# Hard-max attention: three buffers for keys and queries, the next batches' loads and key differences moved to earlier tiles, and one more value gather ahead of the tail

## The chip, the cores and the metric

One core of one Trainium2 chip. The metric is the device time of one execution in microseconds (us), lower is better. A number such as "443.31 us" is the median of several executions on the chip; a "span" is the time from the first to the last instruction of the one execution that was profiled, and is some 2 us shorter. Runs are compared with runs of the kernel before on the same chip and in the same rounds.

## The reference

```python
def setup_inputs():
    B, Sq, Sk, D = 4, 4096, 4096, 128
    # q, k, v: standard normal, float32

def reference(q, k, v):
    logits = np.matmul(q, k.transpose(0, 2, 1))
    best = np.argmax(logits, axis=-1)
    b_idx = np.arange(q.shape[0])[:, None]
    return v[b_idx, best, :].astype(np.float32)
```

For each query: find the key with the largest dot product and copy out that key's value row.

## The kernel before

The queries are worked off in 128 tiles of 128 queries, 32 tiles to a batch. For one tile, PE multiplies queries with sums and differences of keys in groups of four, ACT and DVE fold the results (`W`), and DVE's MAX8 picks the best group (`TOP`). A group holds four keys, so POOL gathers the three *differences* of the group's keys (`kg`, from `k16` in HBM), DVE multiplies them with the query (`prod`) and finds the best of the four. POOL then gathers the value row (`vr`), which SP stores. At the end, queries that were too close to call are worked out again exactly (`FK`, `FQ`, `FV`), and one last scatter writes their rows. All instructions stand in a fixed order for each engine.

Three helpers matter here. They all issue their transfers from POOL, or feed one that does:

```python
natk = [bp.tile([P, 2, 16, P], FP16, ...) for i in range(2)]     # keys of a batch, natural layout
natq = [bp.tile([P, NQT, P], FP16, ...) for i in range(2)]       # queries of a batch

def load_k(b, h, x, y):                                          # float32 in HBM to fp16 in SBUF
    kb = k[b].rearrange("(h p n) d -> p h n d", p=P, n=16)
    nc.gpsimd.dma_start(out=natk[b % 2][:, h, x:y], in_=kb[:, h, x:y])

def put_first(b, h):                       # DVE negates the group's first key; SP writes it three times
    ...
    nc.vector.tensor_scalar(out=kd[:, h, :, 0, :], in0=src[:, :, 0, :], scalar1=-1.0, ...)
    for f in range(3):
        nc.sync.dma_start(out=kb16[:, h, :, f, :], in_=kd[:, h, :, 0, :])

def add_rest(b, h):                        # POOL adds the other three keys to it, in HBM
    ...
    nc.gpsimd.dma_start(out=kb16[...], in_=src[:, :, 1:4, :]..., accum_op=OP.add)
```

and the place of each in the loop over the tiles:

```python
for it in range(T):                        # T = 128
    b, qt = it // NQT, it % NQT            # NQT = 32
    if it < 8:
        load_part(1, it, 4)                # batch 1: keys in 8 pieces of 128 KB
    elif 10 <= qt < 18 and qt % 2 == 0:
        load_part(b + 1, qt - 2)       # next batch: queries in 4 pieces of 256 KB
    elif 18 <= qt < 26 and qt % 2 == 0:
        load_part(b + 2, qt - 18)      # the one after: keys in 4 pieces of 256 KB
    ...
    if it % NQT in (9, 13):
        put_first(it // NQT + 1, it % NQT // 13)
    if it % NQT in (13, 17):
        add_rest(it // NQT + 1, it % NQT // 17)
    ...
    issue(it)                              # how many value gathers POOL issues in this tile
```

`LATE = 4` is the number of value gathers that are issued ahead of the first `FK` of the tail; the rest follow it. Sizes of loads here and below are those of what they write, in fp16.

Of the kernel before, what the change touches and what calls it, by code (L numbers as in the profile page):

```python
# [8 lines left out]
FP16 = mybir.dt.float16  # L9
# [12 lines left out]
TAU = 8.0  # L22
NEAR = 0.5
SLOTS = 6
LATE = 4
NKG = 6


# [1 line left out]
def kernel(ctx, tc, q, k, v, out):  # L30
    nc = tc.nc
    B, Sq, D = q.shape
    Sk = k.shape[1]
    P = 128
    NQT = Sq // P
# [10 lines left out]
    bp = ctx.enter_context(tc.tile_pool(name="kq", bufs=1))  # L46
# [10 lines left out]
    k16 = [dr.tile([Sk, 96], FP16, name=f"k16_{b}") for b in range(B)]  # L57
    kT = [bp.tile([P, Sk], FP16, name=f"kT{i}", tag=f"kT{i}") for i in range(2)]
    qT = [bp.tile([P, Sq], FP16, name=f"qT{i}", tag=f"qT{i}") for i in range(2)]
    natk = [bp.tile([P, 2, 16, P], FP16, name=f"natk{i}", tag=f"natk{i}") for i in range(2)]  # L60
    kd = bp.tile([P, 2, 4, 3, P], FP16, name="kd", tag="kd")
    natq = [bp.tile([P, NQT, P], FP16, name=f"natq{i}", tag=f"natq{i}") for i in range(2)]

    def load_k(b, h, x, y):
        kb = k[b].rearrange("(h p n) d -> p h n d", p=P, n=16)
        nc.gpsimd.dma_start(out=natk[b % 2][:, h, x:y], in_=kb[:, h, x:y])  # L66

    def load_q(b, x, y):
        nc.gpsimd.dma_start(out=natq[b % 2][:, x:y], in_=q[b].rearrange("(p t) d -> p t d", p=P)[:, x:y])  # L69

    def put_k(b, h):
        if b >= B:
            return
        src = natk[b % 2][:, h].rearrange("p (g f) d -> p g f d", f=4)
        nc.vector.tensor_tensor(out=kd[:, h], in0=src[:, :, 1:4, :], in1=src[:, :, 0:1, :].to_broadcast([P, 4, 3, P]),
                                op=OP.subtract)
        kb16 = k16[b].rearrange("(h p n) d -> p h (n d)", p=P, n=16)
        nc.sync.dma_start(out=kb16[:, h], in_=kd[:, h].rearrange("p g f d -> p (g f d)"))

    def put_first(b, h):  # L80
        if b >= B:
            return
        src = natk[b % 2][:, h].rearrange("p (g f) d -> p g f d", f=4)
        nc.vector.tensor_scalar(out=kd[:, h, :, 0, :], in0=src[:, :, 0, :], scalar1=-1.0, scalar2=None, op0=OP.mult)
        kb16 = k16[b].rearrange("(r x) d -> r (x d)", x=4).rearrange("(h p g) (f d) -> p h g f d", h=2, p=P, f=3)
        for f in range(3):
            nc.sync.dma_start(out=kb16[:, h, :, f, :], in_=kd[:, h, :, 0, :])

    def add_rest(b, h):
        if b >= B:  # L90
            return
        src = natk[b % 2][:, h].rearrange("p (g f) d -> p g f d", f=4)
        kb16 = k16[b].rearrange("(r x) d -> r (x d)", x=4).rearrange("(h p g) (f d) -> p h g f d", h=2, p=P, f=3)
        nc.gpsimd.dma_start(out=kb16[:, h].rearrange("p g f d -> p g (f d)"), in_=src[:, :, 1:4, :].rearrange("p g f d -> p g (f d)"),
                            accum_op=OP.add)

    def load_part(b, i, n=8):
        if b >= B:
            return
        if i < 8:  # L100
            load_k(b, i // 4, i % 4 * 4, i % 4 * 4 + n)
        else:
            load_q(b, (i - 8) * NQT // 8, (i - 8 + n // 4) * NQT // 8)

    load_k(0, 0, 0, 16)
    load_q(0, 0, 4)

# [13 lines left out]
    identh = cp.tile([P, P], FP16, tag="identh")  # L121
# [73 lines left out]
    def unit_k(b, i):  # L195
        h, u, y = i // 8, i // 2 % 4, i % 2
        x = 2 * (u // 2)
        ps = pp.tile([P, 256], FP32, tag="u", name=f"uk_{b}_{i}")
        for m in (2 * y, 2 * y + 1):
            o = ps[:, (m - 2 * y) * P:(m - 2 * y + 1) * P]  # L200
            nc.tensor.matmul(out=o, lhsT=natk[b % 2][:, h, 4 * m + x, :], rhs=identh, start=True, stop=False)  # L201
            nc.tensor.matmul(out=o, lhsT=natk[b % 2][:, h, 4 * m + x + 1, :],  # L202
                             rhs=identn if u % 2 else identh, start=False, stop=True)
        c = u * 1024 + h * 512 + y * 256
        nc.scalar.activation(out=kT[b % 2][:, c:c + 256], in_=ps, func=AF.Copy)  # L205

    def turn_q(b, x, y):
        nc.sync.dma_start_transpose(out=qT[b % 2][:, x * P:y * P].rearrange("p (t r) -> p t r", r=P),
                                    in_=natq[b % 2][:, x:y, :].rearrange("p t d -> p (t d)"))

    def trn_q(x, y, put):
        ps = pp.tile([P, 512], FP32, tag="u", name=f"tq_{x}")
# [77 lines left out]
    def dots(c, x, m):  # L290
        c0 = chunks[c][0]
        d = D_t[c % 4]
        b = x // NQT
        gap = ("wait", 1) if m == 4 and x < 200 else ("dve",)
        yield "until", lambda: ("kg", x) in done, 2 if m < 4 and x < TAIL else 1
        kg = kg_t.pop(x)
        prod = rp.tile([P, 4, 3, P], FP16, tag="prod", name=f"prod_{x}")[:, 0:m]
        h = min(m, 2)
        for i in range(0, m, h):
            nc.vector.tensor_tensor(out=prod[:, i:i + h], in0=kg[:, i:i + h],  # L300
                                    in1=natq[b % 2][:, x + i - b * NQT:x + i + h - b * NQT, :].unsqueeze(2).to_broadcast([P, h, 3, P]),
                                    op=OP.mult)
            yield gap
        p1 = rp.tile([P, 4, 3, 64], FP16, tag="p1", name=f"p1_{x}")[:, 0:m]
        nc.vector.tensor_tensor(out=p1, in0=prod[:, :, :, 0:64], in1=prod[:, :, :, 64:128], op=OP.add)  # L305
        yield gap
        p2 = rp.tile([P, 4, 3, 32], FP16, tag="p2", name=f"p2_{x}")[:, 0:m]
        nc.vector.tensor_tensor(out=p2, in0=p1[:, :, :, 0:32], in1=p1[:, :, :, 32:64], op=OP.add)  # L308
        yield "dve",
        nc.vector.tensor_reduce(out=d[:, x - c0:x - c0 + m, 1:4], in_=p2, axis=AX_X, op=OP.add)  # L310
        done.update(("dot", i) for i in range(x, x + m))
# [154 lines left out]
    def flags_last(t0, t1, ready, fill, late):  # L466
# [47 lines left out]

        late(LATE)
        get(FK[:, 0, :], k_flat, gb[:, 0:1], B * Sk)
# [226 lines left out]
    def issue(it):  # L743
        n = 0
        clock[0] = it
        put_out(it)
        behind = len([g for g in near_q if g not in marks]) > (2 if it >= TAIL else 4)
        while near_q and (n < 1 + behind or near_q[0] in marks or it >= T - 1):
            g = near_q.pop(0)
            n += g not in marks  # L750
            g()
        if fast and it >= rest[0]:
            fast.pop(0)()
            rest[0] = it + 2
            n += 1
        if it < 16:
            take_late(2 if n == 0 and len(late_q) > 4 else 1)
            return
        b, qt = it // NQT, it % NQT
        busy = 0.7 if qt % 2 == 0 and (10 <= qt < 18 and b + 1 < B or 18 <= qt < 26 and b + 2 < B) else 0.0  # L760
        if qt in (13, 17) and b + 1 < B:
            busy += 1.0
        rate = 2.42 if it < 72 else 2.5 if it < 100 else 2.42
        room[0] = min(room[0] + rate - busy, 3.0) - n
        for i in range(2):
            if room[0] >= 1 and late_q and it < T - 1:
                take_late(1)
                room[0] -= 1
# [16 lines left out]
            start(flag_segment(0, t + 1, lambda: ("cnt", last) in done, lambda: ("out", last) in done), "flags")  # L785

    TAIL = T - 54
    units = []
    for b in range(1, B):
        x = b * NQT  # L790
        units += [(x - 1, x - NQT + (6 + 3 * i // 2 if b == 1 else 1 + 2 * i), unit_k, b, i) for i in range(16)]
    for it in range(T):
        b, qt = it // NQT, it % NQT
        if it < 8:
            load_part(1, it, 4)
        elif 10 <= qt < 18 and qt % 2 == 0:
            load_part(b + 1, qt - 2)
        elif 18 <= qt < 26 and qt % 2 == 0:
            load_part(b + 2, qt - 18)
        open_units = [u for u in units if u[1] <= it]  # L800
        if open_units:
            u = min(open_units)
            units.remove(u)
            assert it <= u[0]
            u[2](*u[3:])
        if it == 1:
            turn_q(0, 4, 8)
        if it == 40:
            nc.sync.dma_start(out=q32, in_=q[B - 1].rearrange("(p t) d -> p t d", p=P)[:, NQT - 2:NQT])
        if it in (1, 2, 3):  # L810
            turn_q(0, it * 8, it * 8 + 8)
        elif qt >= 16 and qt % 2 == 0 and b + 1 < B:
            turn_q(b + 1, (qt - 16) * 2, (qt - 14) * 2)
        if it > 0:
            screen(it)
        if it >= 1:
            fold(it - 1)
        if it == 1:
            put_k(0, 1)
        if it % NQT in (9, 13):  # L820
            put_first(it // NQT + 1, it % NQT // 13)
        if it % NQT in (13, 17):
            add_rest(it // NQT + 1, it % NQT // 17)
        step(it)
        if it >= 2:
            top(it - 2)
        step(it)
        if it >= 2:
            gathers(it - 2)
        issue(it)  # L830
# [75 lines left out]
```

## Time and profile before

| before | |
|---|---|
| median of 3 executions | 443.31 us (443.29 to 443.79) |
| span of the profiled execution | 441.9 us |
| DVE busy, 45 to 400 us | 353.68 of 355 us |
| transfers issued by POOL | 309 (252 of them gathers of `kg` and `vr`, 34 loads, 6 accumulates) |
| waits of `prod` for a gather | 1, of 0.4 us |
| last MAX8 starts | 405.51 us |
| from there to the final scatter | 32.1 us |
| from the final scatter to the end of the span | 4.2 us |

The prediction below shows the stages and waits, and timelines (start, duration, what, and in brackets idle time before it and what ended it). The groups of POOL's work: line, engine, operation, what it writes from what, count, then busy us in total and mean ns of one, then idle time ahead of it.

```profile
L282 POOL DMA_INDIRECT kg<-k,cand x126 | 126.4, 1003 | 80.0 <-DVE cand L276 48.7 <-issue 29.8 <-DMA vr<-in_v_dram,win 0.6
L342 POOL DMA_INDIRECT vr<-in_v_dram,win x126 | 125.9, 999 | 40.0 <-issue 36.1 <-DVE win L333 1.8 <-DMA vr<-in_v_dram,win 1.2
L66 POOL DMA_DIRECT2D natk<-in_k_dram x19 | 11.3, 599 | 0.8 <-POOLq L890 0.8
L94 POOL DMA_DIRECT2D k<-natk x6 | 8.1, 1352 | 0.0
```

A gather occupies POOL for 1.0 us, a load for 0.6, an accumulate (`k<-natk`) for 1.35. These are the times to *issue* a transfer; the bytes move later, on POOL's one queue (q0 of the trace, 19072 pieces). Then the timeline of POOL at a place that the change touches (start, duration, what, and in brackets idle time before it and what ended it):

```profile
84.56 0.95 POOL L282 DMA_INDIRECT kg<-k,cand  x1 [0.30 <-issue]
85.81 0.97 POOL L342 DMA_INDIRECT vr<-in_v_dram,win  x1 [0.30 <-issue]
86.79 0.60 POOL L66 DMA_DIRECT2D natk<-in_k_dram  x1
87.70 0.98 POOL L282 DMA_INDIRECT kg<-k,cand  x1 [0.30 <-issue]
```

### The profile page before, as it was taken

To read this page: it belongs to the slowest core of one execution; us is meant where nothing else is said; L and a number is where in the kernel's file an instruction comes from. 1 tells how busy PE (TensorE), PEld (TensorE's weight loads), DVE (VectorE), ACT (ScalarE), POOL (GpSimd) and SP (SyncE) were. 2 spreads that over 40 slices of the span, in tenths; PEclk is the share of its full clock that TensorE was granted. 3 is DMA by queue.
4 is the path that set the end of the run, shared out by engine and by line. 5 is a ranking of instruction groups with operands and counts; after the bars stand their busy time and mean duration, and the time that the engine had idled before them with its cause. 6 is when DMAs were issued, how large, how long until landed. Compare 5 with 4: busy or idle time off the path is not lost.

```text
span 441.9 us, 6163 instructions
## 1 busy us (share of the span) xinstructions
PE 378.9 (86%) x1830; PEld 168.0 (38%) x1830; DVE 405.9 (92%) x734; ACT 375.6 (85%) x437; POOL 306.2 (69%) x335
## 2 busy tenths in 40 slices
PE   7999999999999999999998889999889997892100
PEld 4444444444444444444443334443333333330100
DVE  2688999999999999999999999999999999999840
ACT  2899999999999999999998889999989998892000
POOL 8413456677768786777777776777777777777673
PEclk9999999999999999999999999999999999998555
DMA  7933999463326999743336993453322332323432
GB/s 123 202 101 65 157 148 139 106 130 80 108 58 134 180 163 170 147 114 91 84 94 142 173 162 100 96 132 107 85 82 84 90 89 80 88 80 102 122 113 53
DMA packets 52868, 50.54 MB, mean 114 GB/s; under 512 B 34136, under 2 KB 40890, under 8 KB 52832
## 3 DMA queue, kind: packets, MB, share of 16 engines
q0 software_dynamic: 19072, 33.87, 39.2%
q1 hardware_dynamic: 33760, 16.26, 14.5%
q8 instruction: 14, 0.23, 0.2%
q14 instruction: 22, 0.18, 0.2%
HBM read 40.05 MB, written 14.55 MB: 124 GB/s over the span
## 4 chain that ended last, share of the span: by engine, by line
ACT 37%; issue 20%; DVE 13%; PE 12%; POOL 8%; DMA 8%; POOLq 0%; ACTq 0%; DVEq 0%; SPq 0%
ACT A L234 31%; ACT E L247 6%; DVE TOP L264 4%; PE psn L225 4%; POOL vr L342 4%; PE pd L225 4%; POOL kg L282 4%; DVE W L260 4%; PE psn L244 3%; DMA vr<-in_v_dram,win 3%; DMA natk<-in_k_dram 2%; DMA out_dram<-vr 1%; DMA kg<-k,cand 1%; DVE prod L300 1%; DMA vr<-in_v_dram,win_w 1%
## 5 line engine op out<-in xcount | busy, mean ns | idle before, releaser
L234 ACT ACTIVATE A<-pd 128x1024 f16<-128x1024 f32 x256 | 260.8, 1046 | 12.5 <-PE pd L225 12.0
L282 POOL DMA_INDIRECT kg<-k,cand x126 | 126.4, 1003 | 80.0 <-DVE cand L276 48.7
L260 DVE SCALAR_TENSOR_TENSOR W<-psn,E 128x1024 int16<-128x1024 f32 x128 | 167.1, 1306 | 7.4 <-ACT E L247 5.3
L225 PE MATMUL psn<-kT,qT 128*128 128x512 f16 x512 | 151.9, 378 | 11.4 <-ACT A L234 4.0
L225 PE MATMUL pd<-kT,qT 128*128 128x512 f16 x512 | 151.9, 379 | 8.7 <-ACT A L234 8.2
L264 DVE MAX8 TOP<-W 128x8 f32<-128x1024 f32 x128 | 157.0, 1227 | 0.0
L225 PEld LDWEIGHTS <-qT 128*128 128x128 f16 x1024 | 97.9, 97 | 151.8 <-issue 62.0
L342 POOL DMA_INDIRECT vr<-in_v_dram,win x126 | 125.9, 999 | 40.0 <-issue 36.1
L244 PE MATMUL psn<-A,identh 128*128 128x512 f16 x512 | 152.1, 378 | 0.0
L247 ACT ACTIVATE E<-psn 128x1024 int16<-128x1024 f32 x128 | 132.6, 1036 | 2.3 <-PE psn L244 1.5
L244 PEld LDWEIGHTS <-identh 128*128 128x128 f16 x512 | 49.6, 97 | 60.7
L300 DVE TENSOR_TENSOR prod<-kg,natq 128x768 f16<-128x768 f16 x63 | 34.8, 554 | 0.4 <-DMA kg<-k,cand 0.4
L205 ACT ACTIVATE kT<-uk 128x256 f16<-128x256 f32 x48 | 20.6, 429 | 1.5 <-PE uk L202 1.5
L305 DVE TENSOR_TENSOR p<-prod 128x768 f16<-128x768 f16 (+1 forms) x36 | 18.1, 502 | 0.1
L310 DVE TENSOR_REDUCE D<-p 128x12 f32<-128x384 f16 (+1 forms) x36 | 17.7, 492 | 0.1
L201 PE MATMUL uk<-identh,natk 128*128 128x128 f16 x96 | 15.8, 218 | 0.0
L484 PE MATMUL fp_e<-n_e,tri 128*128 128x1 f32 x2 | 0.6, 364 | 13.5 <-DVE n_e L482 13.5
L202 PEld LDWEIGHTS <-natk 128*128 128x128 f16 x96 | 9.3, 97 | 7.2 <-issue 5.1
L308 DVE TENSOR_TENSOR p<-p 128x384 f16<-128x384 f16 (+1 forms) x36 | 11.9, 330 | 0.1
L66 POOL DMA_DIRECT2D natk<-in_k_dram x19 | 11.3, 599 | 0.8 <-POOLq L890 0.8
L201 PEld LDWEIGHTS <-natk 128*128 128x128 f16 x96 | 9.3, 98 | 5.6
L69 POOL DMA_DIRECT2D natq<-in_q_dram x15 | 9.2, 614 | 0.0
(152 smaller groups left out, 140.1 us busy)
## 6 DMA issues: line engine op xcount, KB each, us to landing
out_dram<-vr SPq DMA_DIRECT2D x31, 256.0 KB, 2.1
natq<-in_q_dram POOLq DMA_DIRECT2D x12, 256.0 KB, 5.3
natk<-in_k_dram POOLq DMA_DIRECT2D x10, 256.0 KB, 4.5
k<-kd SPq DMA_DIRECT2D x18, 128.0 KB, 3.7
k<-natk POOLq DMA_DIRECT2D x6, 384.0 KB, 6.4
kg<-k,cand POOLq DMA_INDIRECT x126, 3.0
vr<-in_v_dram,win POOLq DMA_INDIRECT x126, 2.7
natk<-in_k_dram POOLq DMA_DIRECT2D x8, 128.0 KB, 5.7
```

The lines of the kernel that those rows point to most:

```text
L201: nc.tensor.matmul(out=o, lhsT=natk[b % 2][:, h, 4 * m + x, :], rhs=identh, start=True, stop=False)
L205: nc.scalar.activation(out=kT[b % 2][:, c:c + 256], in_=ps, func=AF.Copy)
L225: nc.tensor.matmul(out=ps[:, n * 512:(n + 1) * 512], lhsT=qT[b % 2][:, qt * P:(qt + 1) * P], rhs=kT[b % 2][:, u * 1024 + n * 512:u * 1024 ...
L234: nc.scalar.activation(out=A, in_=ps, func=AF.Abs)
L244: nc.tensor.matmul(out=ps[:, n * 512:(n + 1) * 512], lhsT=identh, rhs=A[:, n * 512:(n + 1) * 512], start=False, stop=True)
L247: nc.scalar.activation(out=E, in_=ps, func=AF.Relu, scale=QSCALE)
L260: nc.vector.scalar_tensor_tensor(out=W_t[t % NW].bitcast(I16)[:, 1::2], in0=ps, scalar=QSCALE, in1=E, op0=OP.mult, op1=OP.max)
L264: nc.vector.max(out=TOP[:, t, :], in_=W_t[t % NW].bitcast(FP32))
L282: near_q.append(lambda j=j: nc.gpsimd.indirect_dma_start(out=kg[:, j].rearrange("p f d -> p (f d)"), out_offset=None, in_=k16[t0 // NQT], ...
L300: nc.vector.tensor_tensor(out=prod[:, i:i + h], in0=kg[:, i:i + h], in1=natq[b % 2][:, x + i - b * NQT:x + i + h - b * NQT, :].unsqueeze(2 ...
L305: nc.vector.tensor_tensor(out=p1, in0=prod[:, :, :, 0:64], in1=prod[:, :, :, 64:128], op=OP.add)
L342: late_q.append(lambda j=j: nc.gpsimd.indirect_dma_start(out=vr[:, j, :], out_offset=None, in_=v_flat, in_offset=IOA(ap=win[:, i + j:i + j ...
```

## The change

The intent: POOL looks loaded from 45 us on and has little to do in the first tiles, so work that can be done early is put there. A third buffer for keys and for queries lets the loads run further ahead. Batch 1 is loaded in four pieces of 512 KB (in tiles 0 to 3) instead of eight of 128 KB (keys) and four of 256 KB (queries); batch 2 is loaded from tile 6 on and batch 3 from tile 24 on, instead of 18 and 50; the negations and accumulates move to earlier tiles; and one more value gather is issued ahead of `FK`.

```diff
-LATE = 4
+LATE = 5
...
-    natk = [... for i in range(2)]
+    natk = [... for i in range(3)]
-    natq = [... for i in range(2)]
+    natq = [... for i in range(3)]
...            (every b % 2 of natk and natq becomes b % 3)
+    plan = {}
+    def load_plan(b, first, gap, n, what):
+        for i in range(32 // n):
+            x, y = i * n, i * n + n
+            plan.setdefault(first + i * gap, []).append(
+                lambda b=b, x=x, y=y: load_k(b, x // 16, x % 16, x % 16 + n) if what == "k" else load_q(b, x, y))
...            (in issue(): busy and rate follow the new places)
+    load_plan(1, 0, 1, 16, "k")
+    load_plan(1, 2, 1, 16, "q")
+    load_plan(2, 6, 2, 8, "k")
+    load_plan(2, 14, 2, 8, "q")
+    load_plan(3, 24, 3, 8, "k")
+    load_plan(3, 44, 4, 8, "q")
...
-        if it < 8:
-            load_part(1, it, 4)
-        elif 10 <= qt < 18 and qt % 2 == 0:
-            load_part(b + 1, qt - 2)
-        elif 18 <= qt < 26 and qt % 2 == 0:
-            load_part(b + 2, qt - 18)
+        for piece in plan.get(it, []):
+            piece()
...
-        if it % NQT in (9, 13):
-            put_first(it // NQT + 1, it % NQT // 13)
-        if it % NQT in (13, 17):
-            add_rest(it // NQT + 1, it % NQT // 17)
+        for b1, x, y in ((1, 5, 9), (2, 17, 21), (3, 38, 42)):
+            for h in range(2):
+                if it == x + 2 * h:
+                    put_first(b1, h)
+                if it == y + 2 * h:
+                    add_rest(b1, h)
```

More of the change, by code (lines that the diff above doesn't have):

```diff
@@ L59 @@
     qT = [bp.tile([P, Sq], FP16, name=f"qT{i}", tag=f"qT{i}") for i in range(2)]
-    natk = [bp.tile([P, 2, 16, P], FP16, name=f"natk{i}", tag=f"natk{i}") for i in range(2)]
+    natk = [bp.tile([P, 2, 16, P], FP16, name=f"natk{i}", tag=f"natk{i}") for i in range(3)]
     kd = bp.tile([P, 2, 4, 3, P], FP16, name="kd", tag="kd")
-    natq = [bp.tile([P, NQT, P], FP16, name=f"natq{i}", tag=f"natq{i}") for i in range(2)]
+    natq = [bp.tile([P, NQT, P], FP16, name=f"natq{i}", tag=f"natq{i}") for i in range(3)]
     def load_k(b, h, x, y):
         kb = k[b].rearrange("(h p n) d -> p h n d", p=P, n=16)
-        nc.gpsimd.dma_start(out=natk[b % 2][:, h, x:y], in_=kb[:, h, x:y])
+        nc.gpsimd.dma_start(out=natk[b % 3][:, h, x:y], in_=kb[:, h, x:y])
     def load_q(b, x, y):
-        nc.gpsimd.dma_start(out=natq[b % 2][:, x:y], in_=q[b].rearrange("(p t) d -> p t d", p=P)[:, x:y])
+        nc.gpsimd.dma_start(out=natq[b % 3][:, x:y], in_=q[b].rearrange("(p t) d -> p t d", p=P)[:, x:y])
     def put_k(b, h):
@@ L73, in put_k @@
             return
-        src = natk[b % 2][:, h].rearrange("p (g f) d -> p g f d", f=4)
+        src = natk[b % 3][:, h].rearrange("p (g f) d -> p g f d", f=4)
         nc.vector.tensor_tensor(out=kd[:, h], in0=src[:, :, 1:4, :], in1=src[:, :, 0:1, :].to_broadcast([P, 4, 3, P]),
@@ L82, in put_first @@
             return
-        src = natk[b % 2][:, h].rearrange("p (g f) d -> p g f d", f=4)
+        src = natk[b % 3][:, h].rearrange("p (g f) d -> p g f d", f=4)
         nc.vector.tensor_scalar(out=kd[:, h, :, 0, :], in0=src[:, :, 0, :], scalar1=-1.0, scalar2=None, op0=OP.mult)
@@ L91, in add_rest @@
             return
-        src = natk[b % 2][:, h].rearrange("p (g f) d -> p g f d", f=4)
+        src = natk[b % 3][:, h].rearrange("p (g f) d -> p g f d", f=4)
         kb16 = k16[b].rearrange("(r x) d -> r (x d)", x=4).rearrange("(h p g) (f d) -> p h g f d", h=2, p=P, f=3)
@@ L95, in add_rest @@
                             accum_op=OP.add)
-    def load_part(b, i, n=8):
-        if b >= B:
-            return
-        if i < 8:
-            load_k(b, i // 4, i % 4 * 4, i % 4 * 4 + n)
-        else:
-            load_q(b, (i - 8) * NQT // 8, (i - 8 + n // 4) * NQT // 8)
+    plan = {}
[4 more added lines that the diff above has]
+                lambda b=b, x=x, y=y: load_k(b, x // 16, x % 16, x % 16 + n) if what == "k" else load_q(b, x, y))
     load_k(0, 0, 0, 16)
@@ L200, in unit_k @@
             o = ps[:, (m - 2 * y) * P:(m - 2 * y + 1) * P]
-            nc.tensor.matmul(out=o, lhsT=natk[b % 2][:, h, 4 * m + x, :], rhs=identh, start=True, stop=False)
-            nc.tensor.matmul(out=o, lhsT=natk[b % 2][:, h, 4 * m + x + 1, :],
+            nc.tensor.matmul(out=o, lhsT=natk[b % 3][:, h, 4 * m + x, :], rhs=identh, start=True, stop=False)
+            nc.tensor.matmul(out=o, lhsT=natk[b % 3][:, h, 4 * m + x + 1, :],
                              rhs=identn if u % 2 else identh, start=False, stop=True)
@@ L208, in turn_q @@
         nc.sync.dma_start_transpose(out=qT[b % 2][:, x * P:y * P].rearrange("p (t r) -> p t r", r=P),
-                                    in_=natq[b % 2][:, x:y, :].rearrange("p t d -> p (t d)"))
+                                    in_=natq[b % 3][:, x:y, :].rearrange("p t d -> p (t d)"))
     def trn_q(x, y, put):
@@ L300, in dots @@
             nc.vector.tensor_tensor(out=prod[:, i:i + h], in0=kg[:, i:i + h],
-                                    in1=natq[b % 2][:, x + i - b * NQT:x + i + h - b * NQT, :].unsqueeze(2).to_broadcast([P, h, 3, P]),
+                                    in1=natq[b % 3][:, x + i - b * NQT:x + i + h - b * NQT, :].unsqueeze(2).to_broadcast([P, h, 3, P]),
                                     op=OP.mult)
@@ L759, in issue @@
         b, qt = it // NQT, it % NQT
-        busy = 0.7 if qt % 2 == 0 and (10 <= qt < 18 and b + 1 < B or 18 <= qt < 26 and b + 2 < B) else 0.0
-        if qt in (13, 17) and b + 1 < B:
+        busy = 0.5 if plan.get(it) else 0.0
+        if it in (42, 44):
             busy += 1.0
-        rate = 2.42 if it < 72 else 2.5 if it < 100 else 2.42
+        rate = 2.45
         room[0] = min(room[0] + rate - busy, 3.0) - n
```

## The prediction

> **What bounds the kernel now.** I began with the page's first two parts, to find the engine that has no room, and then asked for the busy time in five stages: start, filling, first half, second half, tail.
>
> ```profile
> PE 378.9 (86%) x1830; PEld 168.0 (38%) x1830; DVE 405.9 (92%) x734; ACT 375.6 (85%) x437; POOL 306.2 (69%) x335
> ...
> 17.00:45.00 28.00, 27.13 (x133) 12.20 (x132) 23.74 (x24) 28.00 (x34) 6.87 (x9) 1.00 0.55 100
> 45.00:220.00 175.00, 170.96 (x848) 77.05 (x847) 174.54 (x247) 174.54 (x213) 123.55 (x129) 1.00 0.65 126
> 220.00:400.00 180.00, 164.18 (x742) 69.59 (x740) 179.14 (x338) 164.87 (x183) 135.10 (x136) 1.00 0.45 105
> 400.00:442.00 42.00, 2.47 (x12) 1.63 (x10) 23.08 (x114) 0.48 (x1) 25.64 (x26) 0.56 0.33 94
> ```
>
> The lower lines give a stage, its length, then PE, PEld, DVE, ACT and POOL busy time, clock, DMA share and GB/s. From 17 to 45 us ACT never rests (28.00 of 28.00) and DVE has 28.00 - 23.74 = 4.26 us free. From 45 to 400 us DVE is busy 174.54 + 179.14 = 353.68 of 355 us. So DVE sets the pace for four fifths of the run; in 45 to 220 ACT is level with it. POOL, which issues gathers and loads, looks 71 to 75% busy, and the view of waits says what the rest is:
>
> ```profile
> POOL kg L282 <- DVE cand L276: 48.7, 24, 14.4
> POOL vr L342 <- issue: 36.7, 119, 0.8
> POOL kg L282 <- issue: 29.8, 98, 0.3
> ...
> DVE W L260 <- ACT E L247: 5.3, 7, 2.7
> ...
> DVE prod L300 <- DMA kg<-k,cand: 0.4, 1, 0.4
> ```
>
> About 0.3 us of issue stands ahead of each gather, so one takes 1.0 + 0.3 = 1.3 us and POOL is really some 92% occupied in these stages (258.65 us busy and about 235 gathers x 0.3 us, of 355). But it still stops for DVE's candidates 24 times (48.7 us, mostly early; between 120 and 395 us the POOL timeline shows stops of 0.5 to 2.5 us some nineteen times). An engine that stops for its producer is not behind. The last line decides it: of 63 products that read gathered keys, one waited for a gather, 0.4 us. POOL and its transfers do not hold DVE. The page's chain runs through POOL around 220 to 236 and 340 to 380 us; I set that aside, since DVE has no gaps there.
>
> The tail after the last MAX8 (405.5 us) is different; here is POOL's timeline:
>
> ```profile
> 413.88 1.00 POOL L342 DMA_INDIRECT vr<-in_v_dram,win  x1 [0.30 <-issue]
> 417.17 1.05 POOL L512 DMA_INDIRECT FK<-in_k_dram,gb_e  x1 [2.29 <-DVE row_e L509]
> ...
> 422.43 1.00 POOL L342 DMA_INDIRECT vr<-in_v_dram,win  x1 [0.30 <-issue]
> ...
> 431.62 1.00 POOL L342 DMA_INDIRECT vr<-in_v_dram,win_w  x1 [0.30 <-issue]
> 432.92 0.99 POOL L512 DMA_INDIRECT FV<-in_v_dram,xw_fe  x1 [0.30 <-issue]
> 437.69 1.02 POOL L541 DMA_INDIRECT out_dram<-FV,rowk_e  x1 [3.77 <-DMA out_dram<-vr]
> ```
>
> POOL waits 2.29 us for row_e, then issues FK, FQ, FK, FK, six value gathers, the last two and FV back to back, 1.3 us each, and ends with a scatter that waits for the last value rows to be stored. From 417.17 us the tail is POOL's queue: row_e's index starts it, the gathers left over lengthen it. FV's own index was ready at 426.7 us, so FV waits only for the queue.
>
> **What the Trainium skill says.** "Perfetto Trace Analysis", Identifying the Most-Contended Engine, takes the engine of highest occupancy as the one to improve, and its Optimization Strategy adds that a kernel may have regimes with different ones. The stages agree: ACT to 45 us, DVE to 400, POOL's queue at the end. "DMA: Bandwidth & Descriptors", Queues, rings and completion order, says each DMA engine goes round robin between queues a packet at a time, with 9 to 17 descriptors typical in one. The trace's DMA records fit: between 20 and 22 us the transposes' 256-byte pieces (589) and the key loads' 1024-byte pieces (147) passed 4 to 1, i.e. about equal bytes per turn. The same page, SWDGE vs HWDGE vs iDMA, ties casting and accumulating transfers to GpSimd, so these loads cannot simply leave POOL's queue.
>
> **The change part by part.** I compared the order of instructions on each engine, before against after.
> - PE and ACT: the same instructions in the same order. Nothing gained.
> - DVE: the same instructions; only the six `kd` negations of put_first move (tiles 9, 13, 41, 45, 73, 77 to 5, 7, 17, 19, 38, 40). The timeline shows one at 53.07 with its successor at 53.26: 0.19 us of DVE. Four go from one full place to another: 0. The one at 41.17 lies where DVE waits 0.23 us soon after anyway: about 0. The one at 53.07 leaves the full part for about 35 us, where idle time of 0.80 us follows at 39.97: -0.2 us.
> - POOL: key and query loads go from 34 to 26. One costs about 0.6 us (11.3 us for 19, 9.2 us for 15) and follows without an issue gap: 8 x 0.6 = 4.8 us less. After 91 us, POOL had 12 loads and 4 accumulates (1.36 us each), 12 x 0.6 + 4 x 1.36 = 12.6 us; now 7 loads or so and 2 accumulates, 4.2 + 2.7 = 6.9 us. Nearly 6 us leave POOL's crowded part, but by the 0.4 us above they were not on the path. They turn into longer stops for `cand`. At most the single wait near 385 us goes: 0.4 us, half of it counted, -0.2.
> - LATE 4 to 5: one more value gather is issued ahead of FK, one fewer after. The extra one would start at 413.88 + 1.3 = 415.2 and leave POOL free at 416.5, before row_e lets FK start at 417.17. So it fits the 2.29 us hole, FK doesn't move, and everything from 422.43 on comes one slot earlier: FV at 431.6, the scatter at 436.4. -1.3 us on the path that sets the end. The order shows equal work left over (10 value gathers plus 2 in both), so there is no further gain.
> - A third buffer: the loads wait for no earlier reader, but no engine waited for that.
> Sum: -0.2 - 0.2 - 1.3 = -1.7 us, 443.3 - 1.7 = 441.6; I say 441.7.
>
> **Rivals.**
> (a) The start collides. Before, six loads of 128 KB were issued at 13 to 16 us; now four of 512 KB, 2 MB instead of 0.75 MB, in the same queue. The first 512 KB load of the kernel went out at 1.3 us and had landed by 6.6 (semaphore record), some 3.2 us of data, so 2 MB is about 13 us of DMA, from 15 to 28, and with the transposes and key differences (about 6 us) to 33 us. What is needed meanwhile: queries of tiles 4 to 7 landed at 18.8, PE used them at 21.8; queries of tiles 8 to 15 landed at 23.3, used at 33.9; the second half of the differences landed at 24.3, first gather at 30.7. If the turns were one small piece against one 4096-byte piece, the first could land near 22.5 and the second near 33: a stall of 1 to 3 us at the start, which nothing later gives back, so 443 to 445. The 4 to 1 above speaks for turns of equal bytes: then they slip by about 0.5 to 5 us, inside their slack of 3.0, 10.6 and 6.4 us. For it: DMA share was 0.89 already. Against: from 26 to 30 us the engines moved nothing. I give it 12%.
> (b) POOL is the hidden bound and 5 to 6 us of loads taken out of it shorten the run: 436 to 438. For it: the chain through POOL, and issue gaps that make it nearly full. Against: DVE's 353.68 of 355 us and the one 0.4 us wait. 5%.
> (c) POOL's new order makes gathers late. At tiles 16 to 24 POOL now issues loads, two accumulates and gathers almost without a pause. I laid the new order against DVE's times with the durations above: the smallest distance from a gather's landing to its use stays about 0.5 us near 382 us (0.8 in the same estimate of the old order) and 1.8 us near 90 us. So waits of a few tenths at most: +0.3.
> (d) The extra tail gather isn't ready by 415.2 and delays FK by up to 1.3 us, making LATE worth 0. Its index was computed by 412.4 us, so I doubt it.
>
> **Range and chances.** The tail's -1.3 is the firm part; the rest moves by some tenths. With (a) or (d) at the upper and (b) in part at the lower end, 440.6 to 443.3 should hold it 8 times in 10. Two per cent is 8.9 us: (b) would have to give more than it has, and (a) would need three times its worst. Faster 2%, within 2% 95%, slower 3%.
>
> **What would show it.** Right: DVE still busy over 99% from 45 to 400 us; the last MAX8 at 405.0 to 405.6; POOL's idle before FK near 1.0 instead of 2.29; FV near 431.5; the POOL wait for `cand` longer in total than 48.7 us less what the first loads fill. Wrong: PE or DVE waits on `qT`, `kd` or `kg` before 45 us (a); a last MAX8 before 403 us (b); several waits of `prod` on gathers (c); FK later than 417.3 (d).

## More of the kernel before

The gather at 87.70 is that of tile 19, the last of four (tiles 16 to 19) whose `prod` stands in passes 26 and 27 of the loop over the tiles. DVE's timeline shows no bracket at the second `prod`, so the gather is not waited for:

```profile
94.56 0.17 DVE L327 TENSOR_TENSOR sel<-near,iota 128x32 f32<-128x32 f32 x1
94.65 0.55 DVE L300 TENSOR_TENSOR prod<-kg,natq 128x768 f16<-128x768 f16 x1
```

## The result

The changed kernel is correct and slower: **448.19 us** (447.98, 448.05, 448.33, 449.29) against 443.3 us, ratio 1.0116 with a 95% interval of 1.0095 to 1.0136. Ratios here are the mean time of one kernel's fast runs over that of the other's of the same rounds, so not quite the ratio of the medians quoted. Within 2% it is "the same", as predicted; but the prediction was 441.7 with a range of 440.6 to 443.3, and the time lies 4.9 us above that range, on the other side of the kernel before.

The page of the profile after, engines and stages (each row of a stage: its bounds and length, busy us of PE, PEld, DVE, ACT and POOL, the clock, DMA share, GB/s):

```profile
span 446.2 us, 6158 instructions
...
PE 381.3 (85%) x1830; PEld 168.6 (38%) x1830; DVE 406.2 (91%) x734; ACT 376.8 (84%) x437; POOL 302.1 (68%) x327
...
17.00:45.00 28.00, 27.13 (x133) 12.16 (x132) 23.90 (x25) 28.00 (x34) 8.69 (x10) 1.00 1.00 191
45.00:220.00 175.00, 169.91 (x834) 76.12 (x832) 172.12 (x243) 172.91 (x210) 124.60 (x127) 1.00 0.64 126
220.00:400.00 180.00, 164.49 (x745) 69.77 (x743) 179.31 (x335) 165.81 (x185) 127.18 (x129) 1.00 0.34 89
```

The engines are busy as long as before (DVE 406.2 against 405.9), POOL a little less: 302.1 against 306.2, and in the second half 127.18 against 135.10. So the intent was met: about 8 us of POOL's time were taken out of its full part. It bought nothing there, DVE's 179.31 of 180 is what it was. And between 45 and 220 us DVE now has 2.88 us of idle time (175 - 172.12) where it had 0.46 (175 - 174.54). The view of waits says for what:

```profile
POOL kg L282 <- DVE cand L276: 55.5, 23, 15.1
...
DVE prod L300 <- DMA kg<-k,cand: 2.8, 3, 1.8
...
POOL FK L512 <- DVE row_e L509: 1.0, 1, 1.0
```

The freed time of POOL became longer stops for DVE's `cand` (55.5 us, 48.7 before). `FK` waits 1.0 us instead of 2.3, as predicted. But `prod` now waits for gathers three times, 2.8 us in all. DVE's timeline shows the two large ones:

```profile
94.46 0.17 DVE L327 TENSOR_TENSOR sel<-near,iota 128x32 f32<-128x32 f32 x1
96.42 0.56 DVE L300 TENSOR_TENSOR prod<-kg,natq 128x768 f16<-128x768 f16 x1 [1.80 <-DMA kg<-k,cand]
...
156.07 0.56 DVE L300 TENSOR_TENSOR prod<-kg,natq 128x768 f16<-128x768 f16 x1 [0.72 <-DMA kg<-k,cand]
```

and POOL's timeline what stood ahead of the first:

```profile
83.07 1.08 POOL L342 DMA_INDIRECT vr<-in_v_dram,win  x1 [0.30 <-issue]
84.15 1.38 POOL L94 DMA_DIRECT2D k<-natk  x1
85.83 1.22 POOL L282 DMA_INDIRECT kg<-k,cand  x1 [0.30 <-issue]
...
89.58 0.63 POOL L66 DMA_DIRECT2D natk<-in_k_dram  x1
90.51 0.97 POOL L282 DMA_INDIRECT kg<-k,cand  x1 [0.31 <-issue]
```

The gather of tile 19, which `prod` needs in pass 27, is issued at 90.51; before, it was issued at 87.70. And it is used the moment that it lands, at 96.42, 5.9 us after its issue, where the median of such gathers in the kernel before is 3.0 us. Late by 2.8 us and slow by 2.9: that ate the slack and 1.8 us more. The stop in pass 47 is the same in small: an accumulate at 146.93, the gather of tile 39 at 148.63, its use at 156.07.

The records of the single pieces set the two stops apart. At the first, the pieces of both accumulates had gone by 89.3 us, before the gather was issued: they had cost POOL's time ahead of it, and what stood just ahead of it in the queue was the load, whose pieces go from 90.5 to about 93.4 us. At the second, the accumulate's pieces go on until 155.3 us, and the gather lands behind them, at 155.98. And each gather leaves 16 marks when it lands: at the first stop the last mark comes at 96.40, 1.3 us after the one before it (95.06). Six of the eight profiled kernels with early accumulates have this lag of 1.3 us there; the two without it, d2 and d16 below, wait 0.97 and 0.95 us. So more than half of this 1.8 us hangs on one straggling mark, and what holds that back is not shown.

Now the tail of POOL's timeline after:

```profile
417.40 1.02 POOL L342 DMA_INDIRECT vr<-in_v_dram,win  x1 [0.30 <-DVE OH_e L499]
419.39 1.06 POOL L512 DMA_INDIRECT FK<-in_k_dram,gb_e  x1 [0.97 <-DVE row_e L509]
...
433.76 0.99 POOL L512 DMA_INDIRECT FV<-in_v_dram,xw_fe  x1 [0.30 <-issue]
438.64 1.02 POOL L541 DMA_INDIRECT out_dram<-FV,rowk_e  x1 [3.89 <-DMA out_dram<-vr]
```

Counted from the last MAX8 (405.51 before, 407.68 after), `FV` comes at 26.1 instead of 27.4 us and the scatter at 31.0 instead of 32.2: the predicted gain of the tail is there. But look at the last line and the span: before, 441.9 - 437.69 = 4.2 us lie between the start of the final scatter and the end; after, 446.2 - 438.64 = 7.6 us. Nothing is listed in that time, since instructions that only wait are not counted as busy. The raw records of the trace name the one that fills it, POOL's closing DRAIN (an instruction at the end of the program, after which POOL's last few follow):

```
              DRAIN starts   lasts    scatter starts   scatter's bytes land
before        437.46         3.253    437.69           439.8 to 440.0
after         438.41         6.930    438.64           440.7 to 440.9
```

The scatter lands 2.3 us after its start in both. "DMA: Bandwidth & Descriptors", Anatomy of one DMA, in the Trainium skill, gives about 2.0 us as the fixed cost of such a transfer, and the trace agrees with 2.3. So the DRAIN of the kernel after goes on for another 4.4 us when nothing is left to land.

The account of the 4.3 us between the two spans:

| part | before | after | difference |
|---|---|---|---|
| last MAX8 (main stage, waits of `prod`) | 405.51 | 407.68 | +2.17 |
| from there to the scatter | 32.18 | 30.96 | -1.22 |
| from the scatter to the end | 4.19 | 7.55 | +3.36 |
| sum | 441.88 | 446.19 | +4.31 |

The times of the two profiled executions are 443.80 and 447.98 us, the first 0.5 us above its kernel's median, so the first row is known to some tenths only. Of the 3.68 us that the DRAIN grew by, 3.36 reach the end, for before, SP's own closing checks end at 441.05, 0.34 us after POOL's DRAIN.

### The profile page after: what moved, and what is told of

The parts are those of the page before. It is cut to its first block, busy times and chain, and to the rows that moved or that the text cites. A ratio compares the mean times of both kernels' runs of the same rounds, so it can differ in the third digit from the quotient of the medians.

```text
span 446.2 us, 6158 instructions
## 1 busy us (share of the span) xinstructions
PE 381.3 (85%) x1830; PEld 168.6 (38%) x1830; DVE 406.2 (91%) x734; ACT 376.8 (84%) x437; POOL 302.1 (68%) x327
## 4 chain that ended last, share of the span: by engine, by line
DVE 28%; issue 21%; ACT 17%; PE 14%; POOL 10%; DMA 7%; POOLq 0%; ACTq 0%; DVEq 0%; SPq 0%
ACT A L234 14%; DVE TOP L264 12%; DVE W L260 8%; PE psn L225 5%; POOL kg L282 5%; PE pd L225 5%; POOL vr L342 4%; PE psn L244 4%; ACT E L247 4%; DMA kg<-k,cand 3%; DMA natk<-in_k_dram 2%; DVE p L305 1%; DVE prod L300 1%; DMA FK<-in_k_dram,gb_e 1%; DVE p L308 1%
## 5 line engine op out<-in xcount | busy, mean ns | idle before, releaser
L282 POOL DMA_INDIRECT kg<-k,cand x126 | 127.1, 1009 | 86.9 <-DVE cand L276 55.5
L225 PE MATMUL psn<-kT,qT 128*128 128x512 f16 x512 | 151.9, 378 | 10.2 <-ACT A L234 3.8
L190 ACT ACTIVATE kT<-tk 128x512 f16<-128x512 f32 x4 | 2.4, 597 | 7.6 <-PE tk L184 7.6
L66 POOL DMA_DIRECT2D natk<-in_k_dram x13 | 8.0, 615 | 0.8 <-POOLq L894 0.8
```

The source lines that it names most:

```text
L225: nc.tensor.matmul(out=ps[:, n * 512:(n + 1) * 512], lhsT=qT[b % 2][:, qt * P:(qt + 1) * P], rhs=kT[b % 2][:, u * 1024 + n * 512:u * 1024 ...
L282: near_q.append(lambda j=j: nc.gpsimd.indirect_dma_start(out=kg[:, j].rearrange("p f d -> p (f d)"), out_offset=None, in_=k16[t0 // NQT], ...
```

## The experiments

Three questions: (1) are the waits of `prod` the doing of the moved accumulates; (2) is the tail's gain that of `LATE`; (3) what makes the DRAIN long. A fourth came up on the way: the start. "prod waits" below are those on gathers in the profiled run (0: none of 0.15 us or more); "drain" is the end of POOL's DRAIN less the start of the final scatter (3.02 before, 6.70 after); a ratio stands where the run was timed in rounds.

| run | transfers of POOL | median us | ratio to before | prod waits us | last MAX8 | drain us |
|---|---|---|---|---|---|---|
| before | 309 | 443.31 | 1 | 0.4 | 405.51 | 3.02 |
| after | 301 | 448.19 | 1.0116 | 2.8 | 407.68 | 6.70 |
| e1_late5 | 309 | 442.69 | 0.9989 (0.9972 to 1.0005) | 0 | 404.96 | 3.02 |
| e2_old_places | 301 | 446.17 | 1.0069 (1.0052 to 1.0086) | 0.7 | 410.36 | 6.78 |
| e3_small_loads | 309 | 444.15 | 1.0009 (0.9991 to 1.0028) | 3.1 | 408.16 | 2.73 |
| e4_memsets | 301 | 448.81 | 1.0129 (1.0112 to 1.0145) | 2.7 | 407.69 | 6.71 |
| d2_tiny | 303 | 447.26, one run | | 1.5 | 406.57 | 6.74 |
| d4_tiny | 305 | 453.03, one run | | 3.6 | 414.51 | 2.63 |
| d8_tiny | 309 | 444.81 | 1.0035 (1.0018 to 1.0052) | 3.1 | 407.84 | 2.74 |
| d16_tiny | 317 | 445.11, one run | | 2.5 | 407.41 | 3.15 |
| d24_tiny | 325 | 446.11, one run | | 4.6 | 408.65 | 3.80 |
| e5_small_old | 309 | 442.15 | 0.9983 (0.9966 to 0.9999) | 0 | 405.16 | 2.94 |
| f1_big_loads | 301 | 446.50 | 1.0074 (1.0060 to 1.0087) | 0 | 404.86 | 6.58 |
| f2_firsts_early | 309 | 442.03 | 0.9973 (0.9958 to 0.9989) | 0 | 404.82 | 2.94 |
| g40_tiny | 349 | 457.34, one run | | 12.3 | 417.65 | 5.72 |
| g58_tiny | 367 | 467.13, one run | | 19.8 | 425.82 | 7.19 |
| g60_tiny | 369 | 471.93, one run | | 23.0 | 430.51 | 7.35 |
| h60_start | 369 | 566.72, one run, slow chip | | 24.7 | 523.44 | 7.60 |
| h96_tiny | 405 | 491.22, one run, slow chip | | 37.4 | 448.55 | 6.50 |

### LATE alone (e1)

The kernel before with one line changed:

```diff
-LATE = 4
+LATE = 5
```

> The kernel before with LATE 5 alone. All theories: main stage as before (last MAX8 near 405.5 us), FV 1.3 us earlier than 432.92 after that MAX8. Theory C (the closing drain of POOL follows from how many or which DMAs POOL issued): drain about 3.25 us as before, so the time is about 442.0 us, ratio 0.997. Rival L (the drain follows from the fuller queue at the end, LATE 5): drain about 6.9 us, time about 445.7 us.

`FV` came 26.15 us after the last MAX8 (27.41 before, 26.08 after the whole change), the scatter 31.27 (32.18). So the tail's gain belongs to `LATE`, 1.26 us at `FV` and 0.9 at the scatter, which also waits for the last value rows to be stored. In time it is 0.5 us, with an interval that reaches from 1.2 us faster to 0.2 slower. The DRAIN is untouched.

### The negations and accumulates put back (e2)

The kernel after, with `put_first` and `add_rest` in the tiles of the kernel before (9, 13, 17 of each batch):

```diff
-        if it in (42, 44):
+        if qt in (13, 17) and b + 1 < B:
             busy += 1.0
...
-        for b1, x, y in ((1, 5, 9), (2, 17, 21), (3, 38, 42)):
-            for h in range(2):
-                if it == x + 2 * h:
-                    put_first(b1, h)
-                if it == y + 2 * h:
-                    add_rest(b1, h)
+        if it % NQT in (9, 13):
+            put_first(it // NQT + 1, it % NQT // 13)
+        if it % NQT in (13, 17):
+            add_rest(it // NQT + 1, it % NQT // 17)
```

> The changed kernel with the key differences (put_first, add_rest) put back to tiles 9, 13, 17 of each batch. Theory A (the 2.2 us of the main stage come from the accumulating transfers, which hold up gathers at tiles 27 and 47): the waits of prod on gathers go from 2.8 us to under 0.6 and the last MAX8 comes back to about 405.5 us. Rival B (they come from the loads of keys and queries that still stand there): the waits stay near 2.8 us. The closing drain: Theory C expects it to stay near 6.9 us, since the DMAs are the same ones in number.

The waits of `prod` fell from 2.8 to 0.7 us and the median from 448.19 to 446.17 us: two of the lost microseconds are those of the moved key differences. (The edit also moves the place where `issue()` leaves room for an accumulate; f2 below shows that this is not the cause.) The DRAIN stayed long. But the execution that was profiled took 450.85 us, the other four 445.84 to 446.86, and its profile shows a stall that the kernel after had not shown. PE at the start:

```profile
21.06 0.59 PE L244 MATMUL psn<-A,identh 128*128 128x512 f16 x2
25.03 0.64 PE L225 MATMUL pd<-kT,qT 128*128 128x512 f16 x2 [3.38 <-DMA qT<-natq]
```

PE waits 3.38 us for the transposed queries of tiles 4 to 7, which landed at 24.98 us. This is the collision at the start that the prediction had as its first rival. The rows of the stages show its sign, first the kernel after:

```profile
16.00:20.00 4.00, 4.00 (x19) 1.65 (x18) 2.88 (x3) 4.00 (x6) 0.00 (x0) 1.00 1.06 203
```

then this run:

```profile
16.00:20.00 4.00, 4.00 (x19) 1.66 (x18) 2.88 (x3) 4.00 (x6) 0.00 (x0) 1.00 1.72 40
```

The last two columns are DMA share and GB/s. The engines hold transfers more than all the time (their pieces overlap in the records), but move a fifth of the bytes, 40 GB/s instead of 203. The single run d4_tiny had the same stall: PE waited 3.8 us in the same place. Most of its 4096-byte pieces between 15 and 20 us took 2.6 to 5.7 us each, where they take 0.32 us elsewhere. By the fold of tile 16 the two runs were 4.5 and 6.0 us later than the kernel after. They are two of the 26 executions that had the 512 KB loads; none of the 16 timed ones of variants without them lies so far above its fellows, nor any of the 28 of the kernel before on chips of the usual speed. Two cases are few: that the large loads are to blame is likely and not shown, and why the first pieces are so slow stays open.

### The loads of batch 1 in small pieces again (e3)

The kernel after, batch 1 loaded from the same tiles on but in eight pieces of 128 KB (keys) and four of 256 KB (queries):

```diff
-    load_plan(1, 0, 1, 16, "k")
-    load_plan(1, 2, 1, 16, "q")
+    load_plan(1, 0, 0, 4, "k")
+    load_plan(1, 2, 0, 8, "q")
```

> The changed kernel with batch 1's keys and queries loaded in 8 and 4 pieces again instead of 2 and 2, at the same place: 34 loads as before instead of 26. Theory C (drain follows from the count of POOL's DMAs): drain back to about 3.25 us, time about 448.2 - 3.7 = 444.5 us. Rival L: stays 6.9 us, time 448. Main stage as in the changed kernel (last MAX8 near 407.7 us) in either.

The DRAIN fell from 6.70 to 2.73 us and the time by 4 us to 444.15. The waits of `prod` stayed (3.1 us): the two losses are independent of each other. But the edit changes three things at once: the size of the loads, the number of POOL's transfers (309 instead of 301) and that of its instructions. The next runs take these apart.

### Eight more instructions, no more transfers (e4); two to 24 tiny transfers (d2 to d24)

The kernel after with eight memsets on POOL in tile 2, respectively with 2, 4 or 8 tiny loads in tile 4, or 16 or 24 in tiles 4 and 5 (one fp32 row piece of 16 bytes in each partition, into a tile that nothing reads):

```diff
+        if it == 2:
+            for _ in range(8):
+                nc.gpsimd.memset(pad, 0.0)
```

```diff
+        if it == 4:
+            for i in range(8):
+                nc.gpsimd.dma_start(out=pad[:, 4 * i:4 * i + 4], in_=q[0].rearrange("(p t) d -> p t d", p=P)[:, 0, 4 * i:4 * i + 4])
```

> The changed kernel with 8 tiny memsets on POOL while it is idle at the start: as many POOL instructions as before, but 26 loads. If the drain follows from where POOL's instructions end in their fetched blocks (rival F): 3.25 us, time about 444.5 us. If it follows from the DMAs (theory C) or the end of the queue (rival L): 6.9 us, time about 448.2 us.

> The changed kernel with 8 extra loads of 2 KB each on POOL at tile 4, while POOL is idle: 34 loads as before, the four 512 KB loads kept. Theory C1 (the closing drain follows from the number of POOL's transfers or descriptors): drain about 3 us, time about 448.2 - 3.7 = 444.5 us. Rival C2 (it follows from the size of the four large loads): drain stays at 6.9 us, time about 448.2 us.

> The same with 4 extra loads (30). C1: either about 3 us (if the count has to pass a mark between 26 and 30) or 6.9 us (mark between 30 and 34); a value in between (about 5 us) would speak for a cost that shrinks with each transfer. C2: 6.9 us.

> The same with 2 extra loads (28). C1: 3 or 6.9 us by where the mark lies, about 6 us if the cost shrinks with each transfer. C2: 6.9 us.

> The changed kernel with 16 extra tiny loads: 317 POOL transfers. If the drain's length turns on a mark that the count has to pass (between 303 and 305): about 3 us. If it turns on the count's place in a repeating cycle, it can be 3 or 6.9 us; 6.9 would show a cycle.

> The same with 24 extra loads: 325 POOL transfers. A mark: about 3 us. A cycle: 3 or 6.9 us.

The memsets do nothing to the DRAIN (6.71). Eight loads of 2 KB each, which no one needs, shorten it to 2.74 us, and the *added* work makes the kernel 3.4 us faster (448.19 to 444.81) with the large loads still in it. So neither the size of the loads nor the count of instructions sets it, but the number of transfers that POOL issued. The number of pieces on POOL's queue does not set it either: d8 has 18176 of them and e3 19072, with 309 transfers and a DRAIN of 2.7 us in both. But every load that was added or taken out writes 128 rows, one in each partition, so no run tells a count of transfers from a count of rows. And the number does not fix the length wholly: the six runs with 309 have 2.7 to 3.0 us. With two tiny loads (303) it is long, with four (305) short, and from there it rises slowly again: 3.15 us at 317 and 3.80 at 325.

### The kernel before with the large loads only (f1)

```diff
-        if it < 8:
-            load_part(1, it, 4)
-        elif 10 <= qt < 18 and qt % 2 == 0:
+        if it in (0, 1):
+            load_k(1, it, 0, 16)
+        elif it in (2, 3):
+            load_q(1, it * 16 - 32, it * 16 - 16)
+        elif 10 <= qt < 18 and qt % 2 == 0 and b > 0:
             load_part(b + 1, qt - 2)
```

> The kernel before (LATE 4, two buffers, differences where they were) with nothing but batch 1's keys and queries loaded in four pieces of 512 KB in tiles 0 to 3: 301 POOL transfers instead of 309. Theory C1 (drain by the number of POOL transfers): drain 6.9 us instead of 3.25, last MAX8 near 405.5 us, time 443.3 + 3.7 = 447.0 us, ratio 1.008. Rival C3 (the drain belongs to something else in the changed kernel, such as three buffers or its order): drain 3.25, time 443.3 us. By what the runs with large loads showed so far (2 of about 19), some of these executions may be 5 us longer still, by a stall at tile 3 or 4.

This is the test from the other side: two buffers, everything else old, `LATE` 4, but 26 loads and so 301 transfers. The DRAIN is 6.58 us and the kernel 3.2 us slower than before (ratio 1.0074 over five rounds), although its last MAX8 is not late at all (404.86). The third buffer, the moved accumulates and `LATE` have no part in the DRAIN.

### Both repairs (e5), and the negations alone moved (f2)

e5 is e3 and e2 in one: the change with small loads and old places for the key differences. f2 adds only the DVE half of the move to it:

```diff
-        if it % NQT in (9, 13):
-            put_first(it // NQT + 1, it % NQT // 13)
+        for b1, x in ((1, 5), (2, 17), (3, 38)):
+            if it in (x, x + 2):
+                put_first(b1, (it - x) // 2)
```

> The changed kernel with both repairs: batch 1's loads in 8 and 4 pieces, and the key differences back at tiles 9, 13, 17. Theories A and C together: waits of prod on gathers under 0.7 us, last MAX8 near 405.3 us, drain about 3 us, FV 26.1 us after the last MAX8; the time about 443.3 - 1.3 = 442.0 us, level with LATE 5 alone (442.7). If the two costs were not separate, the time stays above 444 us.

> The repaired kernel (small loads, differences at 9, 13, 17) with only the six negations on DVE moved to the changed kernel's tiles 5, 7, 17, 19, 38, 40; the accumulating transfers stay late. Theory A (the accumulates on POOL's queue make gathers late): no wait of prod over 0.7 us, last MAX8 near 405.2 us, time about 442.1 us. Rival A2 (the early negations or their stores do it): waits near 2.8 us at tiles 27 and 47, time about 444.2 us.

e5 takes 442.15 us, 6.0 us less than the kernel after, which is what e2 (2.0) and e3 (4.0) gained one by one: with both repairs the change is a small gain, and no `prod` waits. f2 tells which half of the move had cost: its negations come as early as in the kernel after, its accumulates as late as in the kernel before, and no `prod` waits either. POOL's timeline of f2 around the place where the kernel after waited:

```profile
87.05 0.95 POOL L342 DMA_INDIRECT vr<-in_v_dram,win  x1 [0.30 <-issue]
88.00 0.60 POOL L66 DMA_DIRECT2D natk<-in_k_dram  x1
88.91 0.98 POOL L282 DMA_INDIRECT kg<-k,cand  x1 [0.30 <-issue]
90.44 0.95 POOL L282 DMA_INDIRECT kg<-k,cand  x1 [0.55 <-DVE cand L276]
```

The load stands where it stood in the kernel after, and POOL even has time to stop for `cand` at 90.44. What is gone are the two accumulates ahead of it; from 74 us on, and again ahead of the gather of tile 39, POOL's gathers and loads have the same order in both. So it is the accumulates that make gathers late, not the room that `issue()` leaves for them. f2 is the best version found, **442.03 us, ratio 0.9973** (0.9958 to 0.9989), 1.2 us faster than the kernel before and 6 us faster than the kernel after. That is about what the tail gives.

### Is the DRAIN a cycle? (g40, g58, g60, then h60 and h96)

f2 with one tiny load a tile, from tile 30 on, 40, 58, 60 or 96 of them; and f2 with 60 of them in tiles 4 to 8:

```diff
+        if 30 <= it < 90:
+            nc.gpsimd.dma_start(out=pad[:, it - 30, :], in_=q[0].rearrange("(p t) d -> p t d", p=P)[:, it % 32, 0:4])
```

> The best version so far (309 transfers issued by POOL) with 40 tiny loads, one in each of tiles 30 to 69: 349 transfers. POOL's closing DRAIN was 6.6 to 6.8 us after the scatter's start with 301 to 303 transfers, 2.6 with 305, and then rose by about 0.06 us a transfer to 3.8 with 325. Theory of a cycle of 64 transfers: 2.6 + 44 x 0.06 = 5.2 us. Rival, the count passes one mark near 304 and the drain stays short after it: 3 to 4 us. POOL has room where the tiny loads go (it stops for DVE's candidates), so the last MAX8 should stay within 1 us of 404.9.

> As the run with 40 tiny loads, with 58: 367 transfers. Cycle of 64: the top of the tooth, 2.6 + 62 x 0.06 = 6.3 us, as with 303. One mark: 3 to 4 us.

> As before with two loads more, 60: 369 transfers. Cycle of 64: the drain falls back to 2.6 to 2.9 us, as between 303 and 305. One mark: no difference to 367. A cycle of another length, or a drain that goes by the time and place of the transfers and not by their number: the fall doesn't come between 367 and 369.

Both theories fell. With a cycle of 64, 369 transfers had to give 2.6 to 2.9 us, and gave 7.35; with a single mark, all three had to give 3 to 4 us, and gave 5.72, 7.19 and 7.35. What they show is a straight rise, (7.35 - 3.80) / 44 = 0.08 us for each transfer between 325 and 369.

> The best version with 60 tiny loads as in the run of 369 transfers, but twelve in each of tiles 4 to 8 instead of one a tile from 30 to 89. If POOL's closing DRAIN goes by the number of its transfers: 7.2 to 7.5 us after the scatter's start, as there (7.35). If it goes by how many were issued in the later part of the run, or by how far POOL had fallen behind: 3 to 4 us, as with the 309 without them. The start will stall by 10 us or more, which does not matter for this reading.

> The best version with one tiny load in each of tiles 30 to 125: 405 transfers. The cycle of 64 and the single mark have both fallen (5.72 us at 349, 7.19 at 367, 7.35 at 369). Rise without a fall, 0.08 us a transfer from 369 on: 7.35 + 36 x 0.08 = 10.2 us. A cycle longer than 65 that falls again before 405: well under 7 us. The whole kernel slows by 30 us or more, since gathers wait behind the tiny loads.

With the 60 in the first tiles the DRAIN is 7.60 us, as with the 60 spread (7.35): it is the number that counts, not where in the run they stand. With 405 it is 6.50 us, where the straight rise asks for 10.2: it does fall again, somewhere between 369 and 405. These two runs were on a chip that ran slower at the time, the kernel before took 534.23 us there, so their times are not compared (h96 lies even below that); a gather occupied POOL for 0.95 us there as elsewhere. So the length goes up and falls back more than once, over more than 64 transfers; the length of the cycle, if it is one, and what POOL does in that time, no run shows.

The g runs show one more thing, by accident. The expectation that POOL has room for them missed by far: 60 tiny loads of 2 KB moved the last MAX8 from 404.82 to 430.51. The waits of g60:

```profile
DVE prod L301 <- DMA kg<-k,cand: 23.0, 13, 6.5
```

23 us of waits for gathers, where f2 has none: 25.69 / 60 = 0.43 us of the run for each transfer of next to no size.

## Why the prediction was wrong

By its own steps:

- **DVE sets the pace from 45 to 400 us, and taking loads from POOL there gains nothing.** Right: POOL gave up 8 us in the second half, `cand` stops grew from 48.7 to 55.5 us, DVE's 179.14 of 180 became 179.31.
- **put_first moved: -0.2 us.** Not to be seen: the fold of tile 0 came 0.25 us earlier already, before any negation, and that of tile 16 0.27 us. f2, which moves the negations alone, is level with e5 (442.03 and 442.15).
- **POOL's loads: -0.2 at most.** Nothing to be seen of it; within its size.
- **LATE: -1.3 us.** Right at `FV` (-1.33 from the last MAX8; e1 alone -1.26) and nearly at the scatter (-1.22; e1 alone -0.9). Rival (d), `FK` delayed, did not come: it waits 0.97 us, foreseen as about 1.0.
- **Rival (c), late gathers: "+0.3" at most.** This is the first step that failed. The mechanism was named, the size was seven times too small: 2.17 us in the last MAX8. The waits behind it are undone by e2, e5 and f2. The estimate had put the new order against DVE's times, with each gather landing a fixed time after its issue. The distance of 1.8 us that it found "near 90 us" is where the wait came. The order was right to about that amount; what it lacked is that a gather's transfer is not of fixed length. One took 5.9 us behind a load (1.3 us of it the straggling mark) and one 7.4 us behind an accumulate, instead of 3.0. The trace of the kernel before had such a case: the gather issued at 161.48, next after the accumulate at 159.74, landed at 168.83, 7.4 us later; only nothing waited for it.
- **The end after the scatter** has no step in the prediction at all. It summed to the scatter at 436.4 us and took the 4.2 us behind it as fixed. They became 7.6. This is the largest term, +3.36 us; without it the spans differ by 0.95 us. Nothing in the diff points to it, for it comes from taking eight transfers *out*, which the prediction booked as a small gain; but the span less the final scatter was there as a quantity, and holding it fixed was an assumption that went unsaid.
- **Rival (a), the start, 12%.** It did not strike in the profiled run of the kernel after, but the step that spoke against it was wrong. The prediction read from before, 589 pieces of 256 bytes to 147 of 1024, that turns are of equal bytes. In the kernel after, between 20 and 25 us, 48 pieces of 4096 bytes and 47 to 62 of 256 bytes pass in each us: about one piece against one, and the bytes some 14 to 1. The transposes of tiles 8 to 15 landed at 28.9 us instead of 23.3, the second half of the differences at 29.8 instead of 24.2. Their slack took it. The stall of the two executions out of 26 (4.5 and 6.0 us) was another one: the queries of tiles 4 to 7 came late, while the pieces of the loads were slow in themselves. The Trainium skill's sentence on turns by packets ("DMA: Bandwidth & Descriptors", Queues, rings and completion order) was cited for more than it says: it counts packets and descriptors, not bytes. Why four pieces pass against one there and one against one here, no run shows.
- **Rival (b)**, POOL as the hidden bound, is refuted by the first point; though g60 shows how near it is. Sixty more transfers, and POOL's queue sets the pace.

The sum, as it should have read: -0.25 (the first tiles' offset, unexplained) + 2.34 (waits of `prod`) + 0.08 (not assigned; together +2.17) - 1.22 (tail) + 3.36 (DRAIN) = +4.31 us. The fault that cost most is the missing term behind the scatter, the next the size of rival (c).

## What to carry to other kernels

When a transfer is moved to an earlier place in a queue that also carries gathers, look at the landing time of every gather behind it, not at the busy time of the engine that issues: an accumulating transfer can cost the gathers in the queue more than its 1.4 us of issue (one behind it took 7.4 us instead of 3.0). Compare the time after the last visible instruction in both profiles: a kernel's end may depend on how many transfers an engine has issued, and a fixed closing cost should be measured in each version and not carried over. And where two parts of a change pull in opposite directions, repair them one by one and keep the part that gains: here the smallest part, one gather ahead of `FK`, is the only one whose gain the profiles show.

## What the Trainium skill lacked or had wrong

- No page tells of a closing DRAIN of POOL that lasts microseconds. Here it ends 2.6 to 7.6 us after the start of the last transfer, which lands after 2.3 us; it depends on the number of transfers (or of their rows) that POOL has issued in the whole kernel (6.74 us at 303, 2.63 at 305, 7.35 at 369, 6.50 at 405). It would belong to "DMA: Bandwidth & Descriptors", at the descriptors that GpSimd writes, or to "Perfetto Trace Analysis" at Sequencer-only Instruction, whose diagram has a wait for a semaphore, the execution and the push of a semaphore update, and nothing that depends on transfers.
- "DMA: Bandwidth & Descriptors", Queues, rings and completion order: turns of a packet with 9 to 17 descriptors. In this trace, 256-byte pieces of transposes and 4096-byte pieces of loads pass about one to one (47 to 62 against 48 in a us), 256 against 1024 bytes four to one (589 to 147). The page gives upper bounds for a packet, in its section SWDGE vs HWDGE vs iDMA, but not how many descriptors one holds at which size; that is what a reader needs who puts large loads beside small transfers.
- The same page, Anatomy of one DMA, gives 2.0 us plus bytes by rate for one transfer by itself. It has no word on one that stands behind others in POOL's queue: a gather behind a load took 5.9 us and one behind an accumulate 7.4 us, with a median of 3.0 us, and sixty loads of 2 KB cost 25.7 us of a kernel that was not bound by them.
